# A two-layer trunk of four mixers: the scores of its linear attentions and of its RWKV chunks by halves of the array's rows

## The chip, the cores and the metric

The kernel runs on one core of one Trainium2 chip. The metric is the device time of one execution, in microseconds (us); the engines are TensorE (PE, with PEld for its weight loads), VectorE (DVE), ScalarE (ACT), GpSimd (POOL) and SyncE (SP), which issues most DMAs.

## What is computed

x has 512 tokens and 1024 channels. Each of two layers adds four mixers of 256 channels each, and then a gated feed-forward net:

```python
h = _rms_norm(x, norm_mix_pre[l])
p_a, p_b, p_c, p_d = _split(h @ w_in[l], (RWKV_COLS, GLA_COLS, LRU_COLS, HGRN_COLS))
y_a = _rwkv7_group(p_a, ...)    # delta-rule state, 4 heads of 64
y_b = _gla_group(p_b, ...)      # linear attention, 4 heads, keys of 32, values of 64
y_c = _rglru_group(p_c, ...)    # gated linear recurrence
y_d = _hgrn2_group(p_d, ...)    # linear attention, 4 heads, keys and values of 64
x = x + _rms_norm(jnp.concatenate([y_a, y_b, y_c, y_d], -1) @ w_out[l], norm_mix_post[l])
gate, up = jnp.split(_rms_norm(x, norm_ffn_pre[l]) @ ffn_w_gate_up[l], 2, axis=-1)
x = x + _rms_norm((jax.nn.silu(gate) * up) @ ffn_w_down[l], norm_ffn_post[l])
```

The two linear attentions share one recurrence; within a chunk their scores carry a decay per key channel:

```python
cum = jnp.cumsum(g_c, axis=-2)
diff = cum[:, :, :, None, :] - cum[:, :, None, :, :]
att = jnp.einsum('bhtk,bhsk,bhtsk->bhts', q_c, k_c, jnp.exp(jnp.where(causal, diff, -jnp.inf)))
o = jnp.einsum('bhts,bhsv->bhtv', att, v_c) + jnp.einsum('bhtk,bhkv->bhtv', q_c * jnp.exp(cum), S)
```

## The kernel before

Channels lie on the 128 partitions, tokens along the free dimension, so a tensor of 256 channels is two tiles of 128 x 512, called ct 0 and ct 1. The wide products (w_in, w_out, the feed-forward's two) are the matmuls g of line 398; each weight and each activation is split in a rounded part and a rest, and a product is three or so matmuls of 512 or 256 columns.

**The levels.** `linear()` serves GLA (nh = 4 heads of 32 keys, one tile of keys) and HGRN2 (nh = 2 heads of 64 per tile, two tiles). It builds the 128 x 128 scores of a group of tokens, held keys down and queries across in `att`, by doubling: at level B = 1, 2, 4, ... 64 the queries of every second block of B tokens meet the keys of the block before them. Level 1 is made of products that POOL forms and matmuls with two or four columns (`pp`, line 983; `dk`, line 955, is the diagonal). A level from 2 on goes per tile: ACT makes one copy `qr` of the level's 256 queries per head, scaled by a column `hsel` that is one on that head's key rows and zero on the others (line 994); PE multiplies the keys of all 128 rows with these masked queries (`lv`, line 999), for HGRN2 four matmuls of 128 columns into one PSUM bank, for GLA two banks of two matmuls of 256 columns; DVE copies the bank's valid places into `att` under a mask (line 1005; the last two levels ACT, by plain copies). Behind a level DVE multiplies the queries and the keys by the decay of their block (lines 1017 and 1018), in place. Since an f32 matmul is done in two passes, it shows as two records in the trace: HGRN2's 8 matmuls of a level are 16 records.

**The chunk products.** `rwkv()` has four heads of 64 channels, two to a tile, on rows 0 to 63 and 64 to 127. Line 656 multiplies a head's `bk` and `ar` for each of 8 chunks (64 rows x 128 columns, `A`), four of them into one PSUM bank, head after head, and DVE cuts four pieces out of each bank (lines 661 to 663). Later in `rwkv()`, blocks are transposed, applied and joined (`pq`, `px`, `py`, lines 829 to 843) into chunk outputs `Y` (lines 905 to 911), and Y's mean and variance per head are taken by two matmuls (`mean`, line 916, `var`, line 440) with an ACT step between them (line 918), before the `gate` of line 927.

**PSUM.** Eight banks: three for g (`pg`), three for `A` and most of RWKV (`pr`, taken by `psr`), two for the linear attentions (`pm`, by `psm`).

**The order.** The four mixers and the w_in products that fill PE are five generators, and `merge()` emits instructions by turns from one `yield` to the next. A string of digits per layer, ORDER, says whose turn it is (0 the w_in products, 1 RWKV, 2 HGRN2, 3 GLA, 4 the RG-LRU); what is left when a string ends goes by rates. A scheduler then places the emitted instructions on the engines' queues by its model of their times, so w_out's matmuls can come to stand between the last mixer steps. An engine runs its queue in order.

## Time and profile before

| what | value |
|---|---|
| median of 3 runs | 1410.99 us (1409.94 to 1411.83) |
| the profiled execution | 1410.65 us, of which the span is 1408.9 us |
| PE, PEld, DVE, ACT, POOL busy | 96%, 82%, 56%, 45%, 6% of the span |
| mixers of layer 0 and of layer 1 | about 85 to 290 us and 780 to 985 us of the span |
| line 994 (masked queries) | 96 instructions |

Times in the rows further below are in us from the start of the span. PE's two figures overlap, since a weight load runs beside the matmul before it. PE at 96% is a mean over stages: outside the mixers it is fed without a gap, inside them the stretches differ, and the change touches only the mixers.

### The profile page before, as it was taken

Reading aid. Unit: us, or ns where it says so; the run is one execution under the profiler, and the core shown is the slowest. Engines: PE = TensorE matmul, PEld = TensorE weight load, DVE = VectorE, ACT = ScalarE, POOL = GpSimd, SP = SyncE. Lnnn points to the kernel's source line nnn. Section 1 sums busy time; section 2 is a strip of 40 time slices with the busy share of each in tenths; the row PEclk is TensorE's granted clock in tenths of the full one; section 3 lists DMA queues with packets and bytes.
Section 4 is the critical chain, followed back from the end, with each engine's and each line's share of the span. In section 5 each row is a group of like instructions: output and inputs, shape, how many; then the busy total and the mean of one; then the engine's idle time right before and its main releaser. Section 6 shows DMA issues by size and latency. Waiting matters only on the chain.

```text
span 1408.9 us, 20225 instructions
## 1 busy us (share of the span) xinstructions
PE 1359.2 (96%) x8284; PEld 1150.8 (82%) x8284; DVE 792.9 (56%) x1241; ACT 633.5 (45%) x1035; POOL 81.0 (6%) x71
## 2 busy tenths in 40 slices
PE   7999998999999999999999999989999999999996
PEld 7877877779988888888897778776998888888886
DVE  7598848746834344412666996586286444433234
ACT  6546458555623232322556374676464232223232
POOL 0130102000000000000002300120000000000000
PEclk9989999999999999999999899999999999999999
DMA  7101202314422222433542111133053313233342
GB/s 269 59 30 30 75 16 90 92 46 135 165 90 90 75 90 75 145 91 94 173 149 60 45 45 61 40 96 107 24 171 116 124 45 114 70 101 121 106 130 85
DMA packets 51692, 131.75 MB, mean 94 GB/s; under 512 B 4752, under 2 KB 23776, under 8 KB 51600
## 3 DMA queue, kind: packets, MB, share of 16 engines
q1 hardware_dynamic: 50400, 128.47, 28.5%
q8 instruction: 65, 1.06, 0.3%
q10 hardware_dynamic: 960, 0.95, 0.2%
q0 software_dynamic: 240, 1.05, 0.2%
q14 instruction: 27, 0.22, 0.0%
HBM read 122.06 MB, written 8.39 MB: 93 GB/s over the span
## 4 chain that ended last, share of the span: by engine, by line
PE 79%; DVE 9%; ACT 8%; DMA 2%; issue 2%; POOL 0%; SPq 0%; DVEq 0%; ACTq 0%; POOLq 0%
PE g L398 69%; PE lv L999 2%; DMA block_ws<-in_w_in_dram 1%; DVE block_wl L389 1%; PE nrm L451 1%; ACT block_wh L388 1%; DVE block_att L1005 1%; DMA block_x<-in_xT_dram 1%; PE A L656 1%; PE px L836 1%; ACT block_ws L994 0%; PE ap L742 0%; DVE block_ws L1018 0%; PE pq L829 0%; ACT L1179 0%
## 5 line engine op out<-in xcount | busy, mean ns | idle before, releaser
L398 PE MATMUL g<-block_h,block_wh 128*128 128x512 f32 (+1 forms) x1738 | 496.7, 364 | 9.0 <-ACT block_h L479 7.6
L398 PEld LDWEIGHTS g<-block_h,block_wh 128*128 128x128 f32 x1738 | 317.1, 192 | 61.6 <-ACT block_h L479 8.1
L398 PE MATMUL g<-block_h,block_wl 128*128 128x512 f32 (+1 forms) x1126 | 340.8, 360 | 0.7 <-DVE block_wl L389 0.6
L398 PE MATMUL g<-block_wl,block_wh 128*128 128x512 f32 (+1 forms) x827 | 255.7, 353 | 0.2 <-ACT block_wh L388 0.2
L398 PEld LDWEIGHTS g<-block_h,block_wl 128*128 128x128 f32 x1126 | 210.3, 192 | 32.6 <-DVE block_wl L389 1.9
L388 ACT CAST block_wh<-block_ws 128x1024 fp32r<-128x1024 f32 (+1 forms) x124 | 128.4, 1038 | 226.2 <-DMA block_ws<-in_w_dn_dram 66.2
L398 PE MATMUL g<-block_wl,block_wl 128*128 128x512 f32 (+1 forms) x607 | 184.9, 351 | 0.0
L398 PEld LDWEIGHTS g<-block_wl,block_wh 128*128 128x128 f32 x827 | 151.4, 191 | 22.8 <-ACT block_wh L388 1.0
L389 DVE TENSOR_TENSOR block_wl<-block_ws,block_wh 128x1024 fp32r<-128x1024 f32 (+1 forms) x82 | 102.9, 1257 | 83.6 <-ACT block_wh L388 68.2
L398 PEld LDWEIGHTS g<-block_wl,block_wl 128*128 128x128 f32 x607 | 111.1, 190 | 15.4 <-issue 0.7
L388 ACT CAST block_wl<-block_ws 128x1024 fp32r<-128x1024 f32 (+1 forms) x46 | 47.4, 1031 | 93.6 <-PE g L398 35.4
L398 PE MATMUL g<-block_g,block_wl 128*128 128x512 f32 (+1 forms) x314 | 82.5, 344 | 0.0
L398 PE MATMUL g<-block_g,block_wh 128*128 128x512 f32 (+1 forms) x280 | 81.2, 347 | 0.0
L389 DVE TENSOR_TENSOR block_wl<-block_ws,block_wl 128x1024 fp32r<-128x1024 f32 (+1 forms) x32 | 38.1, 1191 | 50.1 <-ACT block_wl L388 45.8
L398 PEld LDWEIGHTS g<-block_g,block_wl 128*128 128x128 f32 x314 | 53.6, 189 | 7.2 <-issue 0.2
L398 PEld LDWEIGHTS g<-block_g,block_wh 128*128 128x128 f32 x280 | 48.6, 189 | 6.6 <-issue 0.2
L389 DVE TENSOR_TENSOR block_wh<-block_ws,block_wh 128x1024 fp32r<-128x1024 f32 (+1 forms) x29 | 34.6, 1192 | 32.8 <-ACT block_wh L388 27.2
L398 PE MATMUL g<-block_wh,block_wh 128*128 128x512 f32 (+1 forms) x145 | 46.6, 342 | 0.0
L398 PE MATMUL g<-block_wh,block_wl 128*128 128x256 f32 (+1 forms) x133 | 37.9, 337 | 0.4 <-DVE block_wl L389 0.4
L580 POOL TENSOR_SCALAR block_sq<-block_sq 64x512 f32<-64x512 f32 x2 | 1.2, 618 | 579.1 <-DVE block_cum L1250 521.2
L398 PE MATMUL g<-block_h,block_y 128*128 128x512 f32 x90 | 33.7, 389 | 0.0
L398 PE MATMUL g<-block_g,block_h 128*128 128x512 f32 (+1 forms) x100 | 33.0, 366 | 0.0
(1096 smaller groups left out, 2122.1 us busy)
## 6 DMA issues: line engine op xcount, KB each, us to landing
block_ws<-in_w_gu_dram SPq DMA_DIRECT2D x78, 512.0 KB, 3.6
block_ws<-in_w_in_dram SPq DMA_DIRECT2D x48, 512.0 KB, 3.7
block_ws<-in_w_dn_dram SPq DMA_DIRECT2D x39, 512.0 KB, 3.6
block_ws<-in_w_dn_dram SPq DMA_DIRECT2D x18, 384.0 KB, 3.1
xs<-block_x SPq DMA_DIRECT2D x18, 256.0 KB, 3.9
block_x<-xs SPq DMA_DIRECT2D x18, 256.0 KB, 4.0
block_x<-in_xT_dram SPq DMA_DIRECT2D x14, 256.0 KB, 5.3
block_ws<-in_w_out_dram SPq DMA_DIRECT2D x6, 512.0 KB, 3.7
```

What stands on the lines that cost most here:

```text
L388: nc.scalar.copy(out=wh, in_=ws)
L389: nc.vector.tensor_sub(out=wl, in0=ws, in1=wh.bitcast(F32))
L398: nc.tensor.matmul(ps, lhsT=w[:, i, :], rhs=h[i], start=(first and n == 0), stop=(last and n == len(steps) - 1))
L451: nc.tensor.matmul(ps, lhsT=self.ones, rhs=acc[:, s], start=(s == 0), stop=(s == 1))
L580: nc.gpsimd.tensor_scalar(out=low[64:128, :], in0=low[64:128, :], scalar1=0.5, scalar2=0.5, op0=ALU.mult, op1=ALU.add)
L656: nc.tensor.matmul(ps[:, j * P:(j + 1) * P], lhsT=bk[ct][p0:p0 + 64, c_ * P:(c_ + 1) * P], rhs=ar[ct][p0:p0 + 64, c_ * P:(c_ + 1) * P], st ...
L836: nc.tensor.matmul(ps[:, g * P:g * P + P], lhsT=n21[h][:, g * P:(g + 1) * P], rhs=pq[h][:, g * P:g * P + P], start=True, stop=True)
L999: nc.tensor.matmul(ps[:, j * nh * 64:(j + 1) * nh * 64], lhsT=Kt[ct][:, g * P:(g + 1) * P], rhs=qr[:, g].rearrange("p h c -> p (h c)"), st ...
L1005: nc.vector.copy_predicated(out=av[:, :, :, 1, :], mask=m, data=pv)
```

## The change

**Levels.** The 128 rows of keys are split in two halves of 64 rows. Two banks of `pm` are taken at once, one for each half, and the matmuls of a level go by turns: half 0 into the first bank, half 1 into the second (new line 1012). With HGRN2 a half is a head: 16 matmuls of 64 rows and 64 columns, both tiles of keys in one go, that read Q itself; no masked queries are made. With GLA a half holds two heads: 8 matmuls of 128 columns on two masked queries instead of four (new line 1002, by a new constant `hodd`). `att` is kept by halves instead of by tiles. Level 1 and the diagonal of both tiles share one PSUM tile. The branch for B = 2 with PPB, which was not taken, goes.

**Chunk products.** Per tile and per four chunks two `pr` banks are taken, and matmuls alternate between the two heads (new line 657).

**Order.** Both ORDER strings are new. Of line 994's 96 instructions 24 are left (line 1002); ACT loads a function table 41 times instead of 46 (four fewer in layer 0, one in layer 1), as RG-LRU steps that use one table come together. DVE's rows stay about the same (1193 instead of 1195). Matmuls of 64 rows come in 33 runs between others instead of 17. For the most part the halves do alternate; in layer 0 eight matmuls of `lv_5_16` and eight of `lv_5_17` stand one after the other with two `A` between, and GLA's second level of both layers is parted in the same way.

```diff
+    c["hodd"] = (p[:, None] // 32 % 2 == np.arange(2)[None, :])
...
-        for h in range(4):
-            ct, p0 = h // 2, 64 * (h % 2)
-            s_, k_, z_ = self.u("sr"), self.u("sak"), self.u("n21")
+        for ct in range(2):
+            new = [[self.u(n) for n in ("sr", "sak", "n21")] for _ in range(2)]
             for hf in range(2):
-                ps = self.psr("A")
+                pair = [self.psr("A") for _ in range(2)]
                 for j in range(4):
-                    c_ = hf * 4 + j
-                    nc.tensor.matmul(ps[:, j * P:(j + 1) * P], lhsT=bk[ct][p0:p0 + 64, c_ * P:(c_ + 1) * P],
-                                     rhs=ar[ct][p0:p0 + 64, c_ * P:(c_ + 1) * P], start=True, stop=True)
+                    cc = slice((hf * 4 + j) * P, (hf * 4 + j + 1) * P)
+                    for hh in range(2):
+                        rr = slice(64 * hh, 64 * hh + 64)
+                        nc.tensor.matmul(pair[hh][:, j * P:(j + 1) * P], lhsT=bk[ct][rr, cc], rhs=ar[ct][rr, cc], start=True, stop=True)
...
-            for ct in range(ncs if B > PPB else 0):
-                qr = (self.u if nh == 2 else self.u4)("qr").rearrange("p (g h c) -> p g h c", g=4, h=nh)
-                q4 = Q[ct].rearrange("p (g n s b) -> p g n s b", g=4, s=2, b=B)[:, :, :, 1, :]
-                for h in range(nh):
-                    nc.scalar.activation(out=qr[:, :, h, :].rearrange("p g (n b) -> p g n b", b=B), in_=q4, func=AF.Copy, scale=hsel[:, h:h + 1])
-                for bk in range(nbk):
-                    ps = self.psm("lv")
-                    for j in range(tpb):
-                        g = bk * tpb + j
-                        nc.tensor.matmul(ps[:, j * nh * 64:(j + 1) * nh * 64], lhsT=Kt[ct][:, g * P:(g + 1) * P],
-                                         rhs=qr[:, g].rearrange("p h c -> p (h c)"), start=True, stop=True)
...
+                q4 = [z.rearrange("p (g n s b) -> p g n s b", g=4, s=2, b=B)[:, :, :, 1, :] for z in Q]
+                if nh == 4:
+                    qr = self.u4("qr").rearrange("p (g h c) -> p g h c", g=4, h=4)[:, :, 0:2, :]
+                    for h in range(2):
+                        nc.scalar.activation(out=qr[:, :, h, :].rearrange("p g (n b) -> p g n b", b=B), in_=q4[0], func=AF.Copy, scale=self.c("hodd")[:, h:h + 1])
+                ps = [self.psm("lv") for _ in range(2)]
+                for i in range(8 if nh == 2 else 4):
+                    for half in range(2):
+                        rr = slice(64 * half, 64 * half + 64)
+                        ct, g = i // 4, i % 4
+                        if nh == 2:
+                            rhs, out = q4[ct][rr, g], ps[half][:, i * 64:i * 64 + 64].rearrange("p (n b) -> p n b", b=B)
+                        else:
+                            rhs, out = qr[rr, g], ps[half][:, i * P:i * P + P].rearrange("p (h c) -> p h c", h=2)
+                        nc.tensor.matmul(out, lhsT=Kt[ct][rr, g * P:(g + 1) * P], rhs=rhs, start=True, stop=True)
+                for half in range(2):
+                    av = halves[half]
...
                     if lv < 5:
-                        m = self.lmask[:, lv, :].rearrange("p (n b) -> p n b", b=B).unsqueeze(1).to_broadcast([P, 8, nb, B])
-                        nc.vector.copy_predicated(out=av[:, :, :, 1, :], mask=m, data=pv)
+                        nc.vector.copy_predicated(out=av[:, :, :, 1, :], mask=mask, data=pv)
```

The order of the work shows it at three places. The first is ACT in the tail of layer 0, where GLA's levels (the four-fold copies) meet RWKV's copies out of `pq`; L1179 is the RG-LRU's second gelu, with its table load. Before:

```order
L994 ACTIVATE block_ws_77_1593<-block_ws_10_288,cst 128x4x64 x4
L1179 ACT_TABLE_LOAD
L1179 ACTIVATE block_prw_2_4_218<-block_prw_2_4_218 128x512
L994 ACTIVATE block_qr_18_2082<-block_ws_10_288,cst 128x4x64
L831 COPY block_qr_23_1131<-pq_119_2019 128x512
L994 ACTIVATE block_qr_18_2082<-block_ws_10_288,cst 128x4x64 x3
L418 CAST block_y_21_2043<-block_ig_8_1009 128x512
L831 COPY block_qk_5_803<-pq_121_2025 128x512
L831 COPY block_sq_33_146<-pq_123_2069 128x512
L994 ACTIVATE block_qr_21_2122<-block_ws_10_288,cst 128x4x64 x4
L388 CAST block_wh_55_2550<-block_ws_54_2549 128x1024
L831 COPY block_prw_2_4_218<-pq_125_2091 128x512
```

After, at the same levels:

```order
L1002 ACTIVATE block_qr_15_2077<-block_sq_2_284,cst 128x4x64 x2
L418 CAST block_y_21_2057<-block_ig_8_1021 128x512
L834 COPY block_sak_50_1070<-pq_119_2033 128x512
L1002 ACTIVATE block_qr_18_2101<-block_sq_2_284,cst 128x4x64 x2
L834 COPY block_ws_10_288<-pq_121_2039 128x512
L388 CAST block_wh_55_2576<-block_bk_31_828 128x1024
L834 COPY block_prw_2_8_281<-pq_123_2091 128x512
L1002 ACTIVATE block_ws_42_940<-block_sq_2_284,cst 128x4x64 x2
L834 COPY block_prw_2_4_218<-pq_125_2115 128x512
L841 COPY block_sg_14_661<-px_127_2121 128x512
L1002 ACTIVATE block_qr_24_2190<-block_sq_2_284,cst 128x4x64 x2
```

A level has two masked queries instead of four, and the gelu with its load no longer stands among them.

The second place is PE at the end of layer 0, from RWKV's last chunk outputs `Y` on. Before:

```order
L911 MATMUL Y_4_162_2462<-block_n21_4_43_963,block_rs_4_20_676 64x64 x14
L916 MATMUL mean_4_164_2494<-block_ws_2_10_288,cst_75 128x512
L440 MATMUL var_4_166_2497<-block_plr1_3_40_927,cst_75 128x512
L927 MATMUL gate_4_168_2503<-block_sq_1_2_284,lowup_0_44_519 128x512
L398 MATMUL g_0_53_2548<-block_h_0_27_137,block_wh_0_55_2550 128x512
L398 MATMUL g_0_53_2548<-block_h_0_27_137,block_wl_0_56_2551 128x512
```

After, the end of the w_out matmuls that now stand between `Y` and the mean, the mean, and the first of those behind it:

```order
L398 MATMUL g_0_65_2643<-block_wh_3_73_1499,block_wh_0_67_2644 128x256
L398 MATMUL g_0_65_2643<-block_wh_3_73_1499,block_wl_0_68_2645 128x256
L919 MATMUL mean_4_164_2521<-block_pgl5_3_55_1114,cst_75 128x512
L398 MATMUL g_0_75_2708<-block_h_0_27_137,block_wh_0_77_2709 128x256
L398 MATMUL g_0_75_2708<-block_h_0_27_137,block_wl_0_78_2710 128x256
L398 MATMUL g_0_75_2708<-block_wh_3_91_1872,block_wh_0_77_2709 128x256
L398 MATMUL g_0_53_2575<-block_h_0_23_131,block_wh_0_55_2576 128x512
```

Before, mean, variance and gate follow each other; now 20 w_out matmuls stand between `Y` and the mean and 16 between the mean and the variance.

The third place is the same step at the end of layer 1. Before, from the last w_out matmuls ahead of the mean:

```order
L398 MATMUL g_0_464_8050<-block_wl_16_79_6973,block_wh_0_466_8051 128x256
L398 MATMUL g_0_464_8050<-block_wl_16_79_6973,block_wl_0_467_8052 128x256
L916 MATMUL mean_17_164_7922<-block_sq_14_2_5600,cst_75 128x512
L398 MATMUL g_0_474_8115<-block_h_12_2_5384,block_wh_0_476_8116 128x256
L398 MATMUL g_0_474_8115<-block_h_12_2_5384,block_wl_0_477_8117 128x256
L398 MATMUL g_0_474_8115<-block_y_20_19_7408,block_wh_0_476_8116 128x256
L398 MATMUL g_0_474_8115<-block_y_20_19_7408,block_wl_0_477_8117 128x256
```

After:

```order
L398 MATMUL g_0_464_8098<-block_wh_16_83_7060,block_wl_0_467_8100 128x256
L398 MATMUL g_0_474_8163<-block_wh_16_83_7060,block_wh_0_476_8164 128x256
L398 MATMUL g_0_474_8163<-block_wh_16_83_7060,block_wl_0_477_8165 128x256
L919 MATMUL mean_17_164_7971<-block_prw2_15_15_5744,cst_75 128x512
L440 MATMUL var_17_166_7974<-block_ws_0_354_4817,cst_75 128x512
L930 MATMUL gate_17_168_7980<-block_prw2_15_15_5744,lowup_0_437_5956 128x512
L398 MATMUL g_0_446_7998<-block_h_12_12_5518,block_wl_0_428_5356 128x512
```

Here it is the other way round: 16 w_out matmuls stood between mean and variance before, and none does now.

## Rows read from the trace of the kernel before

**Rows 1.** Busy time by stretch, layer 0: start:end, length, engines, PEclk, DMA share, GB/s.
```profile
85.00:112.00 27.00, 24.23 (x110) 19.98 (x109) 27.00 (x41) 9.43 (x17) 11.59 (x7) 0.81 0.09 36
112.00:123.00 11.00, 10.62 (x35) 8.39 (x36) 10.76 (x26) 4.35 (x11) 0.00 (x0) 0.70 0.00 0
...
159.00:200.00 41.00, 40.81 (x334) 32.68 (x336) 25.60 (x46) 18.92 (x35) 0.00 (x0) 1.00 0.17 53
...
226.00:246.00 20.00, 14.83 (x90) 13.21 (x89) 18.36 (x27) 18.36 (x38) 5.51 (x6) 0.91 0.40 132
246.00:265.00 19.00, 18.32 (x257) 16.15 (x256) 16.96 (x38) 7.82 (x14) 0.00 (x0) 1.00 0.31 87
```

**Rows 2.** The same view, layer 1, the two stretches of its tail.
```profile
911.00:929.00 18.00, 12.38 (x75) 9.08 (x74) 14.45 (x21) 13.79 (x25) 11.45 (x11) 0.96 0.45 147
929.00:953.00 24.00, 23.25 (x170) 21.24 (x171) 20.50 (x36) 15.60 (x31) 0.00 (x0) 0.89 0.22 66
```

**Rows 3.** PE timeline, 88 to 130: start, us, engine, line, operation, tiles, shape, count.
```profile
101.46 0.95 PE L955 MATMUL dk<-cst,block_qk 128*128 128x2 f32 x8
102.27 1.03 PE L983 MATMUL pp<-cst,block_qk 128*128 128x2 f32 x8
...
108.75 0.39 PE L398 MATMUL g<-block_h,block_wh 128*128 128x512 f32 x1
109.07 1.16 PE L656 MATMUL A<-block_x,block_x 64*128 64x128 f32 x8
110.15 1.05 PE L983 MATMUL pp<-cst,block_qk 128*128 128x2 f32 x8
...
126.61 0.39 PE L398 MATMUL g<-block_h,block_wl 128*128 128x512 f32 x1
126.84 1.05 PE L999 MATMUL lv<-block_ws 128*128 128x128 f32 x8
127.64 0.71 PE L398 MATMUL g<-block_h,block_wh 128*128 128x512 f32 x2
```

**Rows 4.** PE timeline, 62.4 to 64.6: two 32-row matmuls, each in two passes.
```profile
62.53 0.69 PE L589 MATMUL zw<-block_sq,lowup 32*128 32x512 f32 x1
62.53 0.69 PE L594 MATMUL za<-block_sq,lowup 32*128 32x512 f32 x1
```

**Rows 5.** PE timeline, 827.3 to 828.3: products of heads in different row halves.
```profile
827.40 0.71 PE L656 MATMUL A<-block_ar,block_bk 64*128 64x128 f32 x6
828.04 0.49 PE L999 MATMUL lv<-block_qr,block_ws 128*128 128x128 f32 x2
```

**Rows 6.** PE timeline, 218 to 264: the tail of layer 0, waits in brackets.
```profile
235.50 1.16 PE L829 MATMUL pq<-block_bmat,block_cum 128*128 128x128 f32 x8 [2.09 <-ACT block_qr L831]
...
248.19 1.89 PE L999 MATMUL lv<-block_qr,block_ws 128*128 128x256 f32 x8
249.92 1.05 PE L843 MATMUL py<-block_sq,block_cum 128*128 128x128 f32 x8
```

**Rows 7.** Stretches of both mixers, instructions of L994 alone: busy ACT (count).
```profile
85.00:290.00 205.00, 21.30 (x48) 0.95 0.19 59
780.00:985.00 205.00, 20.97 (x48) 0.96 0.21 68
```

**Rows 8.** ACT timeline, 222 to 262: the tail of layer 0.
```profile
226.74 1.78 ACT L994 ACTIVATE block_ws<-block_ws,cst 128x256 f32<-128x256 f32 x4 [2.56 <-DVE block_ws L1017]
...
232.52 1.28 ACT L1179 ACT_TABLE_LOAD   x1
```

**Rows 9.** DVE timeline, 222 to 262: masked copies and decays of one level.
```profile
251.19 1.30 DVE L1005 COPY_PREDICATED block_att<-lmask,lv 128x512 f32<-128x512 int32 x2
252.41 0.41 DVE L1018 TENSOR_TENSOR block_ws<-block_ws,block_sq 128x256 f32<-128x256 f32 x1
```

**Rows 10.** PE timeline, 279 to 291.5: the end of layer 0, waits in brackets.
```profile
285.44 1.12 PE L916 MATMUL mean<-block_ws,cst 128*128 128x512 f32 x2 [0.69 <-ACT block_ws L913]
288.38 1.12 PE L440 MATMUL var<-block_plr,cst 128*128 128x512 f32 x2 [1.82 <-ACT block_plr L918]
```

More of the change, by code (lines that the diff above doesn't have):

```diff
@@ L43 @@
 CONSTS = [("ident", 128), ("bones", 128), ("cent", 128), ("eye32", 32), ("eye64", 64), ("mnt", 128), ("mn21", 128), ("mak", 128),
[L44 removed]
+          ("mr", 64), ("m4", 32), ("m8", 32), ("m16", 32), ("m32", 32), ("scan", 512), ("hsel", 8), ("hodd", 2)]
 COFF = {}
@@ L97 @@
 KEEP = 0
-PPB = 1
 WIDE = True
@@ L664, in rwkv @@
-                yield
-            sr.append(s_)
-            sak.append(k_)
-            n21.append(z_)
+                for hh in range(2):
+                    s_, k_, z_ = new[hh]
+                    pv = pair[hh].rearrange("p (g s c) -> p g s c", g=2, s=4)
+                    for dst, m in ((nt[ct][:, hh, gg, :], "mnt"), (g4(k_)[:, gg, :], "mak"), (g4(z_)[:, gg, :], "mn21")):
+                        nc.vector.tensor_tensor(out=dst, in0=pv[:, :, 1:3, :].rearrange("p g s c -> p g (s c)"), in1=bc(self.c(m), 2), op=ALU.mult)
+                    nc.vector.tensor_tensor(out=s_.rearrange("p (g s c) -> p g s c", g=NPAIR, s=2)[:, gg], in0=pv[:, :, 0:4:3, :],
+                                            in1=self.c("mr").unsqueeze(1).unsqueeze(1).to_broadcast([P, 2, 2, 64]), op=ALU.mult)
+                    yield
@@ L669, in layouts @@
+            for s_, k_, z_ in new:
+                sr.append(s_)
+                sak.append(k_)
+                n21.append(z_)
         def layouts(ct):
@@ L946, in linear @@
         ncs = len(Q)
-        nbk = 1 if nh == 2 else 2
-        tpb = 4 // nbk
-        att, tots, tst, prod = {}, [], [], []
+        att, tots, tst, prod = [], [], [], []
+        by_half = lambda z: z.rearrange("p (h j) -> p h j", h=2)
+        if nh == 2:
+            place = lambda z, ct, g: by_half(z)[:, :, ct * 4 + g]
+        else:
+            place = lambda z, ct, g: by_half(z)[:, :, g * 2:g * 2 + 2]
+        pd = self.pm.tile([P, 16], F32, tag="pm", name=self.nm("dk"))
         for ct in range(ncs):
@@ L952, in linear @@
             nc.gpsimd.tensor_mul(out=qk[:, 0], in0=Q[ct], in1=Kt[ct])
-            pd = self.pm.tile([P, 4, nh], F32, tag="pm", name=self.nm("dk"))
             for g in range(4):
-                nc.tensor.matmul(pd[:, g, :], lhsT=qk[:, 0, g * P:(g + 1) * P], rhs=hsel, start=True, stop=True)
+                nc.tensor.matmul(place(pd, ct, g), lhsT=qk[:, 0, g * P:(g + 1) * P], rhs=hsel, start=True, stop=True)
             prod.append(qk)
-            dk = self.sp.tile([P, 4 * nh], F32, tag=f"dk{nh}{ct}", name=self.nm("dk"))
-            nc.scalar.copy(out=dk, in_=pd.rearrange("p g h -> p (g h)"))
-            for bk in range(nbk):
-                t = self.u4("att").rearrange("p (j c) -> p j c", c=P)
-                nc.gpsimd.tensor_tensor(out=t, in0=self.c("ident").unsqueeze(1).to_broadcast([P, 8, P]),
-                                        in1=dk[:, bk * 8:bk * 8 + 8].unsqueeze(2).to_broadcast([P, 8, P]), op=ALU.mult)
-                att[ct, bk] = t
             nc.vector.tensor_mul(out=Q[ct], in0=Q[ct], in1=F[ct])
@@ L966, in linear @@
             tst.append(self.u("tots"))
+        dk = self.sp.tile([P, 16], F32, tag=f"dk{nh}", name=self.nm("dk"))
+        nc.scalar.copy(out=dk, in_=pd)
+        for half in range(2):
+            t = self.u4("att").rearrange("p (j c) -> p j c", c=P)
+            nc.gpsimd.tensor_tensor(out=t, in0=self.c("ident").unsqueeze(1).to_broadcast([P, 8, P]),
+                                    in1=dk[:, half * 8:half * 8 + 8].unsqueeze(2).to_broadcast([P, 8, P]), op=ALU.mult)
+            att.append(t)
+        yield
+        if nh == 2:
             yield
@@ L990, in linear @@
[L990 to L1002 removed]
+            halves = [att[half].rearrange("p j (n s b) -> p j n s b", s=2, b=B) for half in range(2)]
```

49 lines of the change are left out of this document (21 added, 28 removed).

## The prediction

> **What bounds the kernel now.** I read the busy times by stretch first, since PE's mean of 96% hides the mixers. In layer 0 the limit changes [rows 1]: from 85 to 112 us DVE is busy 27.00 of 27 us, from 112 to 123 again 10.76 of 11; from 159 to 200 PE is busy 40.81 of 41; from 226 to 246 DVE and ACT are busy 18.36 each of 20 and PE only 14.83; from 246 to 265 PE has 18.32 of 19 and DVE 16.96. In layer 1 [rows 2], from 911 to 929 nothing is full (PE 12.38, DVE 14.45, ACT 13.79 of 18), which means that single waits in a chain set the time; from 929 to 953 PE is busy 23.25 of 24. So PE time is worth something where PE is full, ACT time where ACT is in the chain, and DVE, whose work the change leaves as it is, caps both: a stretch can't get shorter than its DVE time. Then I read PE's rows for the price of a pass, and ACT's, DVE's and PE's waits in the tails.
>
> **What a matmul costs.** In an f32 matmul of 128 columns a pass takes 0.11 us: eight of `dk` start at 101.46 and what follows at 102.27, so 0.81 for 8, and eight of `lv` stand from 126.84 to 127.64, 0.80 [rows 3]. `dk` moves two columns, `lv` 128, and the price is the same; what a pass of this kind pays is thus the load of 128 weight columns, not the columns that it moves. With 256 moving columns eight passes take 249.92 - 248.19 = 1.73, 0.216 each [rows 6]. Whether two row halves overlap is the question of the change. The two 32-row matmuls `zw` and `za`, on different rows and banks, both start at 62.53 and both last 0.69 [rows 4]; and six records of `A` that join two heads take 828.04 - 827.40 = 0.64 us [rows 5], no more than six full passes (0.66) though they are 64-row work, which alone takes 110.15 - 109.07 = 1.08 for 8, or 0.135 [rows 3]. I take a pair of halves to cost one pass, 0.11.
>
> A visit to the 64-row form has a price: 8 `A` take 1.08 where 8 `lv` take 0.80, so 0.28, and the `g` ahead of them is left after 0.32 (108.75 to 109.07) where it is left after 0.23 (126.61 to 126.84), so 0.09 [rows 3]; 0.37 together, for 16 more visits 5.9 us. The Trainium skill has a rule that speaks against the change here: "TensorEngine Tiling (Array Packing)", section Key Properties, says that changing the tiling mode drains the TensorE. The trace agrees with a price for it, 0.37 us by the rows, and I charge it by the rows.
>
> **PE's account.** HGRN2: 16 records of 0.11 = 1.76 us a level become 16 pairs of 0.11 = 1.76: nothing gained; where halves don't alternate it loses, some 2.5 us for the runs that I count in the new order. GLA: 8 records of 0.216 = 1.73 become 8 pairs of 0.11 = 0.88, so -0.85 for each of 12 levels of both layers, less for the three that are parted: 9 x 0.85 = -7.7. `A`: the 64 matmuls of both layers are 128 records, which become 64 pairs; 64 passes fewer at 0.80 / 8 = 0.10: -6.4. Visits +5.9. The sum is -5.7 us of PE. What counts is where.
>
> **ACT's account.** Line 994 is busy 21.30 us for 48 copies and 20.97 for 48 [rows 7], 0.44 each; 72 fewer are -31.6 us. Five table loads fewer at 1.28 [rows 8] are -6.4. Most of the 38 us lie in stretches where ACT isn't the limit.
>
> **Where it lands, layer 0.** 85 to 123: DVE is full, so `A` and HGRN2's copies are worth nothing; 0. 123 to 226: PE is full and gets nothing back from HGRN2; `A`'s half of 6.4 stands against eight visits (+3.0) and parted halves; 0. One table load lies on the chain of waits late in this part (ACT carries it from 200 to 226): -1.3. 226 to 246: ACT makes 20 copies here, half of which go, 10 x 0.44 = 4.4, with the gelu's load 5.7; PE waits 2.09 for ACT in it [rows 6], and a level's four copies take 1.78 [rows 8]. DVE's 18.36 of 20 caps it at -1.6. 246 to 265: three GLA levels, 3 x 0.85 less 3 x 0.37 = -1.4 (DVE's cap would be -2.0). After that, PE waits 0.69 for the mean's input and 1.82 for the variance's [rows 10]; the new order puts 20 and 16 w_out matmuls there, so -2.5. Layer 0: -1.3 - 1.6 - 1.4 - 2.5 = -6.8.
>
> **Layer 1.** The front as in layer 0: 0. 911 to 929: two of four copies (-0.9) and one table load (-1.3) of the chain: -2.2, within DVE's slack of 3.55. 929 to 953: PE full, four GLA levels, -3.4, four visits, +1.5: -1.9. At the end the same 16 matmuls have left the place between mean and variance, so the wait of 1.82 that layer 0 loses arises here: +1.8. Layer 1: -2.3.
>
> The sum is -9.1, from the profiled execution's 1410.65: 1401.5 us. The median of the runs, 1410.99, is 0.3 above that execution, so the forecast for the median is the same within its own error.
>
> **What can't be read.** Halves with 64 moving columns, alternating for 16 matmuls, no row shows. From below: a pair could cost as little as half a pass (0.055), from above two passes (0.22); the nearest row is `A` joining two heads [rows 5], which is one pass, and this I take. Reading Q with a stride instead of a packed copy I put at nothing, since passes are bound by the load; if it isn't, it costs at most the price of 0.216 of a pass with twice the columns. DVE's copies keep their shapes, 0.65 us each [rows 9].
>
> **Rivals.** *More of ACT counts.* If the chains through ACT are shortened by their full savings and DVE's stretches shrink as well since its inputs come earlier: three more table loads of layer 0 (-3.9), four copies more per tail, -5 each: 1401.5 - 14 = about 1387.5. For it speaks the wait of 2.56 us ahead of the copies at 226.74 [rows 8], against it DVE's full stretches [rows 1]. Chance 0.13.
>
> *HGRN2's levels halve, too.* If two halves of 64 rows load and move at once and 64 columns are cheaper than 128, a pair costs 0.055, and 12 levels gain 12 x 0.88 = -10.6, of which I let all count: about 1391. `dk` with two columns at the full 0.11 [rows 3] speaks against it. The Trainium skill, "TensorEngine Tiling (Array Packing)", section Theoretical Speedup, gives up to 2x where the contraction is 64 or less; by that rule, if it came on top of the columns, it would be this case. Chance 0.04.
>
> *Absorbed.* The tails are bound by DVE and by RWKV's own chain, and each saved wait is taken up by the next: only the waits at the end of layer 0 and a table load are won, less the one at the end of layer 1: -2, 1408.5. For it speaks DVE at 18.36 of 20 and 16.96 of 19 [rows 1]. Chance 0.19, of which 0.08 within 0.2%.
>
> *Slower: the HGRN2 level as one piece.* Before, the first bank of a level is done after half its matmuls (0.88 us), its mask copy runs beside the second half, and Q's decay waits only for the ACT copy, since PE reads `qr`. Now both banks end with the last pair (1.76), and the decays of Q (0.41 each [rows 9]) wait for the matmuls as well. The two copies and the decays are at the head of DVE's queue, where DVE is the full engine (85 to 123): RWKV's cuts of `A` and w_in's subtractions are queued behind. Price 0.88 + 2 x 0.41 = 1.7 us a level, 12 levels: +20, so 1421. It turns the result into a loss from 1.0 us a level on (12 x 1.0 = 9.1 + 2.8). Against it: the order has two streams more to put between, and the level's place was chosen anew. Chance 0.12.
>
> *Slower: halves don't overlap.* If the halves run one behind the other, an HGRN2 level costs 32 x 0.11 = 3.52, +21 us in all, GLA's -7.7 and `A`'s -6.4 are gone: some 1436. The rows of `zw`, `za` and of `A` across two heads speak against it [rows 4, 5]. Chance 0.03.
>
> **How the numbers follow.** A measurement of this kernel can tell about 0.2%, 2.8 us. The forecast, 1395 to 1407, has 0.49; more of ACT 0.13, HGRN2 halved 0.04, absorbed 0.19, the two slower ones 0.15. Faster by over 0.2% (below 1408.2): 0.49 + 0.13 + 0.04 + 0.11 = 0.77, less 0.02 for forecasts that end short of it: 0.75; within: 0.08 + 0.02 = 0.10; slower: 0.15. The range takes in the case of more ACT (1387.5) and the absorbed one (to 1412) and leaves the slower ones out.
>
> **What would show it.** In PE's timeline two `lv` of different halves start a few ns apart and an HGRN2 level lasts 1.76 us, a GLA level 0.88. ACT has 24 masked queries and 41 table loads. The tails shrink (226 to 265 by about 3 us, 911 to 953 by about 4), 159 to 200 stays; the wait ahead of `var` is gone in layer 0 and is 1.8 in layer 1. I would be wrong if pairs cost over 0.15, if DVE's waits for PE at the mask copies grow by over a us per level, or if the front of the mixers, where I expect nothing, moves by several us.

## The result: slower by half a per cent, where a gain was forecast

The changed kernel takes 1417.09 us (median of 15 runs, 1414.37 to 1425.83), the kernel before 1410.99 (15 runs beside them). The ratio is 1.0059 with an interval of 1.0046 to 1.0072: slower, about 8 us in the mean, where 9.1 us less were forecast. The changed kernel's runs lie at 1414 to 1419 us or at 1422 to 1426, the latter at a lower mean clock (0.970 to 0.971 instead of 0.974 to 0.980). The profiled execution took 1415.45 us, span 1413.6; the one of before 1410.65, span 1408.9.

The stretches of [rows 1, 2] in the changed kernel; the columns are start:end, length, busy time (and count) of PE, PEld, DVE, ACT and POOL, then PEclk, DMA share and GB/s:

```profile
85.00:112.00 27.00, 22.18 (x121) 18.19 (x120) 26.86 (x43) 6.07 (x9) 9.77 (x6) 0.87 0.21 75
112.00:123.00 11.00, 10.50 (x58) 8.19 (x58) 10.77 (x24) 1.45 (x2) 0.00 (x0) 0.84 0.01 1
159.00:200.00 41.00, 41.00 (x371) 33.49 (x370) 20.86 (x38) 16.83 (x30) 0.00 (x0) 1.00 0.13 40
226.00:246.00 20.00, 15.74 (x117) 14.17 (x116) 17.52 (x24) 11.66 (x25) 9.36 (x10) 0.91 0.32 105
...
929.00:953.00 24.00, 18.08 (x142) 16.89 (x141) 20.00 (x35) 11.88 (x24) 4.81 (x7) 0.75 0.14 42
```

ACT did fall where the copies were: 226 to 246 shows 11.66 us instead of 18.36. DVE is as full at the front as before. The last stretch now has PE at 18.08 of 24 and a clock of 0.75, where [rows 2] had 23.25 and 0.89. But equal times hold different work in the two kernels. For equal work I cut each layer in two: from the first w_in matmul of a layer's mixers to its last (the front), and from there to an equal place behind the mixers (the tail). PE's busy time of before in these four pieces, then of the changed kernel:

```profile
84.34:226.10 141.76, 137.01 (x889) 0.94 0.13 42
226.10:329.28 103.18, 94.00 (x900) 0.98 0.27 83
749.91:917.40 167.49, 163.39 (x984) 0.97 0.15 50
917.40:1009.13 91.73, 82.62 (x813) 0.96 0.23 72
```

```profile
84.47:228.90 144.43, 137.80 (x969) 0.92 0.14 44
228.90:329.64 100.74, 92.02 (x965) 0.98 0.26 78
751.11:921.20 170.09, 161.47 (x1081) 0.97 0.15 46
921.20:1013.83 92.63, 81.70 (x860) 0.93 0.21 66
```

In short windows PEclk reads either 1.00 or 0.50, the upper and the lower of its two levels (2.4 and 1.2 GHz). As an estimate, half of the busy time at the lower one is time that the clock took: six `g` of 512 columns from 139.40 to 141.96, at the lower level, take 0.43 us each, 24 from 163.54 on, at the upper, 0.24. I subtract it from the busy time and call the rest work:

| piece | elapsed | PE idle | taken by the clock | PE work |
|---|---|---|---|---|
| layer 0 front | 141.76 to 144.43 | 4.75 to 6.63 | 8.26 to 11.95 | 128.75 to 125.86 |
| layer 0 tail | 103.18 to 100.74 | 9.18 to 8.72 | 1.71 to 1.64 | 92.30 to 90.38 |
| layer 1 front | 167.49 to 170.09 | 4.10 to 8.62 | 5.12 to 4.18 | 158.27 to 157.29 |
| layer 1 tail | 91.73 to 92.63 | 9.11 to 10.93 | 2.91 to 3.87 | 79.71 to 77.84 |
| sum | 504.16 to 507.89 | 27.13 to 34.91 | 18.00 to 21.63 | 459.04 to 451.35 |

PE's work shrank by 7.7 us, more than the 5.7 forecast. It came back as 7.8 us more of waiting and 3.6 more at the lower clock: +3.7 us in the mixers, of the span's +4.7. A second profiled execution of the changed kernel (1418.97 us) has nearly the same work, 450.24, but 35.83 of waiting and 24.89 for the clock: 510.96 us in the mixers, +6.8.

**The prices are right.** PE of the changed kernel: start, duration, line, tiles, shape, count.

```profile
123.39 1.16 PE L657 MATMUL A<-block_ar,block_bk 64*128 64x128 f32 x16
124.48 0.73 PE L398 MATMUL g<-block_h,block_wh 128*128 128x512 f32 x2
...
161.61 1.11 PE L1012 MATMUL lv<-block_prw,block_ws 64*128 64x64 f32 x16
162.55 1.06 PE L1012 MATMUL lv<-block_pm 64*128 64x64 f32 x16
163.54 1.66 PE L398 MATMUL g<-block_h,block_wh 128*128 128x512 f32 x6
...
248.13 1.16 PE L1012 MATMUL lv<-block_qr,block_ig 64*128 64x128 f32 x16
249.22 1.16 PE L846 MATMUL py<-block_sg,block_cum 128*128 128x128 f32 x8
```

Sixteen records of `A` take 124.48 - 123.39 = 1.09, where eight took 1.08 [rows 3]. An HGRN2 level of 32 records takes 163.54 - 161.61 = 1.93 (1.76 forecast, without the way in), a GLA level 249.22 - 248.13 = 1.09 instead of 1.73 [rows 6], forecast 0.88 and 0.37 for the visit. ACT's masked copies (start:end, length, busy time of that line) fell from 21.30 and 20.97 us [rows 7] to

```profile
85.00:290.00 205.00, 5.49 (x12) 0.93 0.21 65
780.00:995.00 215.00, 5.47 (x12) 0.94 0.20 62
```

**The waits are new.** What PE waited for in the fronts of layer 0 and of layer 1 (engine, tile, line, releaser: us in all, times, longest):

```profile
PE lv L1012 <- DVE block_att L994: 2.4, 1, 2.4
PE dk L962 <- POOL block_qk L960: 1.9, 1, 1.9
PE lv L1012 <- DVE block_att L1017: 1.3, 2, 1.2
...
PE lg L1167 <- DVE block_att L994: 2.3, 1, 2.3
PE lv L1012 <- DVE block_att L1017: 1.5, 1, 1.5
PE lg L1167 <- DVE block_att L1017: 0.7, 1, 0.7
```

Lines 994 and 1017 are DVE's masked copies out of a `pm` bank. `lv` and `lg` don't read `att`; what they wait for is the bank. The five rows with `att` are 8.2 us (7.7 in the second execution); in the mixers of before no wait of PE that the view lists ended on a mask copy. They took the place of other waits (in layer 0's front before, 1.17 for a cut of `A` and 1.08 for a decay), so idle time rose by less.

Ahead of the first of them DVE, which is full here, stands still for two instructions beside HGRN2's diagonals of `att`, which POOL now forms one right behind the other (timelines of POOL and of DVE):

```profile
100.03 4.19 POOL L971 TENSOR_TENSOR block_att<-cst,dk 128x1024 f32<-128x1024 f32 x2
100.06 2.41 DVE L1161 SCALAR_TENSOR_TENSOR block_sq<-block_rs,vec,block_sq 128x511 f32<-128x511 f32 x1
102.39 2.91 DVE L389 TENSOR_TENSOR block_wh<-block_cum,block_wh 128x1024 fp32r<-128x1024 f32 x1
```

Instructions of these lines take 0.74 and 1.22 elsewhere in the front, so DVE lost 3.4 us. Before, it lost about as much beside the same two products, but 14 us apart.

In the tails the largest wait is now, in layer 0 and in layer 1,

```profile
PE pq L832 <- DVE block_cum L811: 4.3, 1, 4.3
...
PE pq L832 <- DVE block_phg L811: 5.9, 1, 5.9
```

The timeline of all engines of the changed kernel shows what made `pq` wait in layer 0 (waits in brackets):

```profile
232.19 0.56 POOL L826 COPY block_sq<-block_prw 64x256 f32<-64x256 f32 x1
...
232.41 4.34 DVE L1029 TENSOR_TENSOR block_sq<-block_sq,block_m 128x256 f32<-128x256 f32 x1
...
232.72 1.89 POOL L971 TENSOR_TENSOR block_att<-cst,dk 128x1024 f32<-128x1024 f32 x1
...
234.57 1.89 POOL L971 TENSOR_TENSOR block_pm<-cst,dk 128x1024 f32<-128x1024 f32 x1
236.67 1.17 DVE L811 COPY block_cum<-block_sak 32x256 f32<-32x256 f32 x4
...
237.99 0.77 PE L832 MATMUL pq<-block_qk,block_cum 128*128 128x128 f32 x2 [4.26 <-DVE block_cum L811]
```

The decay of 232.41 normally takes 0.41 us. It takes 4.34, and ends at 236.75, 0.3 us behind POOL's two broadcast products, GLA's diagonals of `att` (234.57 + 1.89 = 236.46). `pq`'s four copies stand behind it on DVE's queue. The Trainium skill, "SBUF — State Buffer", section Who interferes with whom, says that a DVE instruction with two inputs in SBUF contends with a GpSimd instruction that reads SBUF, and that the second to issue is blocked until the first is through. The trace agrees: POOL's copy of line 826 had been running for 0.22 us when the decay started, the two products followed it, DVE got no turn between them, and 0.41 us became 4.34.

In the kernel before layer 0's `pq` copies came ahead of the diagonals; in layer 1 the same stop was there already, and the forecast had not read it (timeline of before):

```profile
923.46 4.27 POOL L961 TENSOR_TENSOR block_att<-cst,dk 128x1024 f32<-128x1024 f32 x2 [3.31 <-issue]
923.99 4.49 DVE L808 COPY block_qr<-block_qr 32x256 f32<-32x256 f32 x4
...
928.62 0.77 PE L829 MATMUL pq<-block_bmat,block_qr 128*128 128x128 f32 x2 [4.12 <-DVE block_qr L808]
```

### The profile page after: what moved, and what is told of

Same layout as the page of the kernel before. It is cut to its first block, busy times and chain, and to the rows that moved or that the text cites. A ratio compares the mean times of both kernels' runs of the same rounds, so it can differ in the third digit from the quotient of the medians.

```text
span 1413.6 us, 20724 instructions
## 1 busy us (share of the span) xinstructions
PE 1355.2 (96%) x8572; PEld 1146.9 (81%) x8572; DVE 790.9 (56%) x1241; ACT 596.4 (42%) x956; POOL 78.8 (6%) x71
## 4 chain that ended last, share of the span: by engine, by line
PE 80%; DVE 11%; ACT 5%; DMA 2%; issue 1%; POOL 1%; SPq 0%; DVEq 0%; POOLq 0%; ACTq 0%
PE g L398 70%; PE lv L1012 2%; PE nrm L451 1%; PE pq L832 1%; DMA block_ws<-in_w_in_dram 1%; DVE block_wl L389 1%; DMA block_x<-in_xT_dram 1%; PE px L839 1%; DVE block_wh L389 1%; DVE block_att L1017 0%; DVE block_tots L1033 0%; PE ms L440 0%; PE o L1059 0%; ACT block_wh L388 0%; PE ap L745 0%
## 5 line engine op out<-in xcount | busy, mean ns | idle before, releaser
L398 PE MATMUL g<-block_h,block_wl 128*128 128x512 f32 (+1 forms) x960 | 290.9, 369 | 0.3 <-DVE block_wl L389 0.3
L398 PEld LDWEIGHTS g<-block_h,block_wl 128*128 128x128 f32 x960 | 184.1, 194 | 30.9 <-issue 1.4
L398 PE MATMUL g<-block_wl,block_wh 128*128 128x512 f32 (+1 forms) x710 | 204.3, 359 | 0.0
L398 PE MATMUL g<-block_g,block_wh 128*128 128x512 f32 (+1 forms) x415 | 120.8, 347 | 0.0
L398 PE MATMUL g<-block_wh,block_wh 128*128 128x256 f32 (+1 forms) x395 | 117.0, 332 | 0.4 <-DVE block_wh L389 0.4
L398 PE MATMUL g<-block_wl,block_wl 128*128 128x512 f32 (+1 forms) x358 | 108.1, 351 | 0.0
L398 PEld LDWEIGHTS g<-block_wh,block_wh 128*128 128x128 f32 x395 | 71.6, 191 | 7.8 <-DVE block_wh L389 0.6
L398 PEld LDWEIGHTS g<-block_wl,block_wl 128*128 128x128 f32 x358 | 65.8, 189 | 9.2 <-issue 0.2
L398 PE MATMUL g<-block_wh,block_wl 128*128 128x256 f32 (+1 forms) x240 | 72.5, 331 | 0.0
L398 PEld LDWEIGHTS g<-block_wh,block_wl 128*128 128x128 f32 x240 | 44.5, 190 | 4.9 <-issue 0.8
```

Source lines behind the costliest of these rows:

```text
L398: nc.tensor.matmul(ps, lhsT=w[:, i, :], rhs=h[i], start=(first and n == 0), stop=(last and n == len(steps) - 1))
```

## The experiments

**Parts of the change alone.** Four kernels take one part each, a fifth the new code with the old order.

```diff
 e1  before, with
+    pair = [self.psr("A") for _ in range(2)]     # and the loop over both heads of line 657
 e2  after, with linear() of before for HGRN2 (nh == 2)
 e3  after, with linear() of before for GLA (nh == 4)
 e4  before, with
-ORDER = ('0111101111011010210121241120...
+ORDER = ('0111101110111010210121241122...
 x   after, with the ORDER of before
```

The recorded expectations name theories. Theory 1, later B, is the HGRN2 level as one piece; theory 2, later A, is DVE standing still beside POOL's diagonals; theory 3 is the order strings. Theory C has the clock fall where the levels move few columns, theory D behind waits of PE.

> The kernel before with the chunk products of two heads alternating over two banks, and nothing else (old levels, old order string). Theory 1 (the HGRN2 level as one piece costs the time in the front of the mixers): the pairs are a pure gain of PE in stretches where DVE is the limit, so 0 to -4 us against before. Theory 2 (DVE is held up at the two diagonals formed by POOL, ahead of RWKV's blocks): the same, 0 to -4 us. Theory 3 (the new order string loses the time): 0 to -4 us. Above +2 us would say that the pairs themselves cost, for instance because two pr banks are held at once.

> The changed kernel with HGRN2's levels as before (masked queries, one tile at a time); pairs of chunk products, GLA by halves and the new order string stay. Theory 1 (HGRN2 as one piece): the loss in the front, 2.7 us in each layer, goes and the gain of GLA's levels stays: -5 to -9 us against before. Theory 2 (DVE held up at GLA's diagonals): the front comes back, the wait of pq (4.3 and 5.9 us in the changed kernel) stays: 0 to -4 us. Theory 3 (the order string): still +3 to +6 us.

> The changed kernel with GLA's levels as before (four masked queries, 256 columns); pairs of chunk products, HGRN2 by halves and the new order string stay. Theory 1 (HGRN2 as one piece): the loss in the front stays, the gain in GLA is gone: +6 to +12 us against before. Theory 2 (DVE held up at GLA's diagonals): those are formed in the same way, and GLA's old levels add 5 to 10 us in the tails: +5 to +12 us; if the wait of pq shrinks below 2 us here, theory 2 falls. Theory 3: +3 to +8 us.

> The kernel before, whole, with the new order strings alone. Theory 1 (HGRN2 as one piece) and theory 2 (DVE held up): within 3 us of before, since neither cause is in it. Theory 3 (the order string): +4 us or more.

> The new code with the old order strings. If each string fits only the code it was made for, as the old code with the new strings (+2.4%) suggests: +10 to +35 us against before. If the new code is better by itself and its new strings cost time: below the changed kernel, 1400 to 1412.

| kernel | median us | ratio to before |
|---|---|---|
| e1, chunk products alone | 1431.18 | 1.0161 (1.014 to 1.0183) |
| e2, GLA's levels and the chunk products | 1448.22 | 1.0275 (1.026 to 1.0291) |
| e3, HGRN2's levels and the chunk products | 1441.93 | 1.0218 (1.0185 to 1.0251) |
| e4, new order alone | 1443.10 | 1.0236 (1.0214 to 1.0258) |
| x, all but the new order | 1448.23 | 1.028 (1.0261 to 1.0299) |

Each is at least 14 us worse than either whole kernel, so none prices a part. The expectations for e1 to e3, between -9 and +12 us of before, were missed by far (22, 39 and 33); e4 came out as theory 3 has it (34), and x above its range (39). By e4 and x an order string fits only the code that it was made for. In e1 one and the same edit did nearly all of its harm in layer 1: ACT's table load of line 436 that comes some 290 us behind a layer's mixers is 1.0 us later than before in layer 0 (583.21 for 582.22) and 20.8 in layer 1 (1299.37 for 1278.59). Likewise x: its PE work in the mixers is 451.36, like the changed kernel's 451.35, but its idle time is 47.52 instead of 34.91 and the clock takes 43.60 instead of 21.63. All other experiments therefore freeze the order: the rows of each queue are recorded from the unedited kernel and imposed on the edited one, so that an edit changes durations and waits alone (where it takes an instruction to another engine or behind others, the text says so). Each result below is the median in us and the ratio to the kernel before, run beside it, with the 95% interval. The changed kernel itself, run again beside them, gives 1418.90, ratio 1.0062 (1.0045 to 1.0078):

> The changed kernel as it is, on the chip of this call, as the measure for the runs with its order kept: 1.004 to 1.008 of before, mean granted clock 0.975. A ratio below 1.003 would take the ground from the gain put down to the late diagonals and the doubled columns.

**Is the slower rival right, the HGRN2 level as one piece?** If the decays and mask copies behind a level's matmuls are what costs, it must help to let the matmuls read a constant instead of Q and K.

```diff
-rhs = q4[ct][rr, g];  lhsT = Kt[ct][rr, g * P:(g + 1) * P]
+rhs = f4[ct][rr, g];  lhsT = self.c("scan")[rr, g * P:(g + 1) * P]     # f4: the same view of scan; HGRN2 only
```

> The changed kernel, order kept, in which HGRN2's level matmuls read a constant instead of the decayed queries and keys (so no matmul waits for a decay and no decay for a matmul; the banks and the mask copies stay). Theory B (HGRN2's levels as one piece): the waits in the front go, -5 to -9 us against the changed kernel, to about 1408 to 1412. Theory A: within 2 us of the changed kernel. Theory C: within 2 us.

> The same edit in the kernel before, order kept: HGRN2's masked copies and level matmuls read a constant. Theory B: the levels were loose already, 0 to -2 us against before. Theory A and C: within 2 us of before. If it falls by as much as the same edit gives in the changed kernel, theory B falls.

After: 1417.97, 1.0058 (1.0043 to 1.0073), as without the edit, where theory B expected -5 to -9 us; before: 1409.21, 0.9989 (0.9975 to 1.0003). One half of this rival, which ended on the right side, is refuted: that decays and matmuls wait for each other costs nothing that can be measured in the changed kernel. The other half, mask copies that come only when both banks are done, the edit leaves as it is: PE's waits that end on a mask copy are still 7.8 us in the mixers.

**Do halves overlap?** Here both halves, of the levels and of `A`, go through rows 0 to 63.

```diff
-rr = slice(64 * half, 64 * half + 64)
+rr = slice(0, 64)
```

> The changed kernel, order kept, with all level matmuls and chunk products on rows 0 to 63 (the second half of keys is left out and the first taken twice), so that no two halves can run together. If pairs cost one pass by overlapping, PE's work rises by 12 x 1.76 for HGRN2, 12 x 0.88 for GLA and 64 x 0.11 for the chunk products, 39 us together, and the time by 25 to 40 us against the changed kernel. If the halves don't overlap, nothing changes. By theory D the time at the lower clock changes little.

1451.98, 1.03 (1.0276 to 1.0325). A level (PE timeline of this run):

```profile
174.64 2.00 PE L1012 MATMUL lv<-block_prw,block_ws 64*128 64x64 f32 x16
176.48 1.95 PE L1012 MATMUL lv<-block_pm 64*128 64x64 f32 x16
178.36 0.36 PE L745 MATMUL ap<-block_nst,block_m 128*128 128x32 f16 x8
```

178.36 - 174.64 = 3.72 instead of 1.93. So the overlap is real; that part of the forecast holds. PE's work in the mixers rises by 28 us to 479.41, less than the 39 expected; the clock takes 44.50 instead of 21.63 and PE waits 22.07 instead of 34.91. So not all of the 35 us is the price of a pass, and theory D, by which the clock would have changed little, is not borne out here.

**What is ACT's saving worth?** In the kernel before, the copies are made for one group of four only:

```diff
-out=qr[:, :, h, :], in_=q4          rhs=qr[:, g]
+out=qr[:, 0:1, h, :], in_=q4[:, 0:1]    rhs=qr[:, 0]
```

> The kernel before, order kept, with ACT's masked copies cut to one group of four (64 columns instead of 256; the level matmuls read that group for all four). It asks what ACT's saving alone is worth, with nothing else changed: 96 copies get shorter by 0.15 to 0.3 us, 15 to 29 us of ACT. By the prediction's account 2 to 5 us of that reach the end; by the rival in which all of ACT's saving in the tails counts, 6 to 12 us; if DVE and RWKV's chain absorb it, 0 to 1 us.

1404.31, 0.9965 (0.9949 to 0.9981): 5 us less, in the order of before and with nothing else changed. The copies got only 0.10 us shorter each (0.44 to 0.34), 10 us of ACT in all, so about half of what ACT saved reached the end.

**POOL's diagonals.** In both kernels (f3 after, f4 before) ACT writes the diagonal's place by a plain copy, and POOL's product goes.

```diff
-nc.gpsimd.tensor_tensor(out=t, in0=ident, in1=dk, op=ALU.mult)
+nc.scalar.copy(out=t, in_=ident)
```

> The changed kernel with every instruction in its old place on every queue, except that the eight diagonals of the scores are formed by ACT as plain copies of the unit matrix (the factor dk is left out) instead of by POOL. Theory A (DVE stands still while POOL forms the diagonals; in the trace one decay of 0.4 us takes 4.34 us beside them, ahead of RWKV's blocks): the wait of pq shrinks from 4.3 and 5.9 us to about 1 and 2, and the time falls by 5 to 8 us against the changed kernel, to about 1408 to 1412. Theory B (HGRN2's levels now run as one piece, copies and decays waiting for both banks): within 2 us of the changed kernel. Theory C (the slower clock in the front and the tail): within 2 us.

> The same edit in the kernel before, order kept: diagonals by ACT as copies of the unit matrix. Theory A: DVE is held up less there, since a layer's two HGRN2 diagonals were formed 14 us apart and pq's inputs came ahead of GLA's: 0 to -4 us against before, clearly less than the same edit gives in the changed kernel. Theories B and C: within 2 us of before.

After: 1407.11, 0.9994 (0.9974 to 1.0015), about 9 us better than the changed kernel (5 to 8 expected); before: 1405.93, 0.997 (0.9957 to 0.9982), 4 us better than its own. The place of layer 0 in f3's timeline:

```profile
228.29 0.62 DVE L1032 TENSOR_TENSOR block_sq<-block_sq,block_m 128x256 f32<-128x256 f32 x1
...
228.84 1.18 DVE L811 COPY block_cum<-block_sak 32x256 f32<-32x256 f32 x4
...
231.30 3.33 PE L832 MATMUL pq<-block_qk,block_cum 128*128 128x128 f32 x16
```

The decay takes 0.62 instead of 4.34 and `pq` doesn't wait. PE's idle time in the mixers falls from 34.91 to 23.43 us. The waits that end on a mask copy fall with it, from 8.2 to 4.3 us; the two for level 1's copies, 2.4 and 2.3, become 0 and 0.4. So a good part of them goes with the diagonals, and is not the price of the banks alone. Yet the front of layer 1 keeps 8.33 us of idle time, of 8.62. The profiled execution of f3, 7 us above its median, shows part of that given back to the clock (34.29 us). Between f3 and f4, both without the diagonals, the change still costs 0.9994 - 0.997 = 0.24%, 3.4 us, no more than the two intervals leave open.

If DVE makes the diagonals itself, nothing is won:

```diff
-nc.gpsimd.tensor_tensor(out=t, ...)
+nc.vector.tensor_tensor(out=t, ...)
```

> The changed kernel, whole, order kept, with the diagonals formed by DVE instead of POOL (nothing left out). Theory A (DVE is held for the whole of POOL's 4 us): DVE pays 2 x 1.2 us at each of the four places instead of standing still for 3 to 4 us, so -1 to -5 us against the changed kernel. If POOL's work was free beside DVE's: +2 to +8 us.

1417.92, 1.0061 (1.0046 to 1.0076), where -1 to -5 us were expected. Idle time is 30.71 us instead of 34.91 and 35.83 in the changed kernel's two profiled executions, but the clock takes 30.22 instead of 21.63 and 24.89.

Next only the time of GLA's diagonals moves: they wait for `pq`'s copies, and in layer 1 stand behind the POOL copies of lines 825 and 826. The same in the kernel before (h1).

```diff
+for i in gla_diagonals:
+    for e in pq_copies:      # line 811, in h1 808
+        tc.add_manual_dep(i, e.name, ...)
```

> The changed kernel, whole, order kept but for GLA's two diagonals of each layer: POOL forms them only after DVE has made the copies that pq needs (in layer 1 also after POOL's own copies for RWKV). Theory A (DVE held beside the diagonals): pq starts 3 to 4 us earlier in each layer; in layer 1 GLA's first mask copies now wait for the late diagonals, so 1 to 2 us come back: -3 to -7 us against the changed kernel, to about 1410 to 1414. If the place of the hold doesn't matter (it only meets DVE's work elsewhere): within 2 us of the changed kernel.

> The kernel before, whole, order kept, with GLA's diagonals waiting for the copies that pq needs. In layer 0 those copies come first anyway; in layer 1 they lie beside the diagonals and take 4.49 us instead of 1.2, so theory A expects -2 to -3.5 us against before (1406 to 1407.5). If the hold only meets other work of DVE: within 1 us of before.

After: 1414.59, 1.0036 (1.0019 to 1.0053), some 3.5 us better, an effect hardly larger than the intervals; `pq`'s wait falls from 4.26 to 0.54 us in layer 0 and from 5.9 to 1.6 in layer 1. Before: 1408.48, 0.9995 (0.9984 to 1.0006), no difference that can be told, where theory A expected -2 to -3.5 us, although the copies now take 1.17 instead of 4.49 us. The wait only moves on: PE waits 0.80 instead of 4.12 us for `pq`, but then 2.06 at the next half of a GLA level, for a mask copy that itself waits for the late diagonal (DVE in h1's timeline).

```profile
921.87 1.17 DVE L808 COPY block_qr<-block_qr 32x256 f32<-32x256 f32 x4
...
925.21 1.33 DVE L990 COPY_PREDICATED block_att<-lmask,pp 128x512 f32<-128x512 int32 x1 [1.44 <-POOL block_att L961]
```

**The clock.** In the changed kernel the clock falls twice among HGRN2's levels in layer 0. Four stretches of PE (length, busy, PEclk, DMA share, GB/s):

```profile
128.80:135.50 6.70, 6.70 (x43) 0.99 0.00 0
135.50:142.30 6.80, 6.80 (x28) 0.50 0.00 0
142.30:152.50 10.20, 8.88 (x90) 1.00 0.33 104
152.50:159.30 6.80, 6.80 (x32) 0.50 0.24 77
```

A run of levels and `A` begins in the first at 131.91, the levels end at 136.86; in the third a level follows on a wait of 1.15 us. PE is never idle in the second or the fourth. Two kernels let an HGRN2 matmul move 128 columns instead of 64: f7 all tokens of a group, f7b each column twice.

```diff
 f7
-rhs, out = q4[ct][rr, g], ps[half][:, i * 64:i * 64 + 64]
+rhs, out = Q[ct][rr, g * P:(g + 1) * P], ps[half][:, o:o + P]     # o = min(i * 64, 384)
 f7b, for i < 7
+rhs, out = q4[ct][rr, g].unsqueeze(1).to_broadcast([64, 2, nb, B]), ps[half][:, i * 64:i * 64 + P]
```

> The changed kernel, order kept, in which HGRN2's level matmuls move 128 columns instead of 64 (all queries of the group; what they write beyond their 64 columns is written over or left wrong). By the rows a pass is bound by its 128 weight columns, so the passes should keep 0.11 us a pair. Theory C (the granted clock falls because the new levels feed the array half as many columns in the same time): the time at the lower clock falls from 51 us in the mixers towards 38 us, the mean clock rises from 0.975 to 0.98 or more, and the time falls by 3 to 8 us against the changed kernel. Theory D (the clock falls behind waits of PE, not for what the matmuls carry): clock and time as in the changed kernel, within 2 us. If the passes get longer, by 12 levels of 16 pairs, the time rises by up to 20 us.

> The changed kernel, whole, order kept; HGRN2's level matmuls move their 64 columns twice (the second 64 are written over by the next matmul of the same half, the last one moves 64). It repeats the run with 128 columns without leaving anything wrong. Theory C (the clock falls where the levels feed few columns): mean clock 0.977 to 0.98 and -2 to -5 us against the changed kernel. Theory D (the clock falls behind waits alone): within 2 us, clock 0.975.

f7: 1414.72, 1.0039 (1.0027 to 1.0052). f7b: 1414.50, 1.0043 (1.0029 to 1.0058). Mean clock of the runs 0.9787 and 0.9792, against 0.9748 and 0.9758 for the changed kernel (15 and 4 runs) and 0.983 for the one before. A level costs nearly the same (f7: from 160.25 to 162.24, 1.99 us, against 1.93), and the first of the two falls is gone, while the second stays (f7b, PE):

```profile
128.40:135.10 6.70, 6.70 (x51) 1.00 0.00 0
135.10:141.90 6.80, 6.80 (x57) 1.00 0.01 2
...
147.25:154.08 6.83, 5.09 (x46) 0.50 0.38 146
```

Around the second, f7b's PE waits 2.42 us for DVE (line 735) and 1.74 for a mask copy. The edit brings 2.5 us, an effect about as large as the intervals: layer 0's front has 13.65 us at the lower level instead of 23.89, but 10.24 us of idle time instead of 6.63 in f7.

Late diagonals and doubled columns together:

> The changed kernel, whole, with both edits: late GLA diagonals and HGRN2's columns moved twice. If theories A and C hold and their gains add: -6 to -11 us against the changed kernel, 1406 to 1411, which is at or below the kernel before. If the clock gives back what the waits save, as when DVE formed the diagonals: -2 to -5 us.

1412.63, 1.0023 (1.0014 to 1.0032), clock 0.9813: 5 us better than the changed kernel and still slower than the one before. Only kernels that leave work out (f1, f4) were measurably faster than the kernel before.

## Why the prediction was wrong, point by point

- **Price of a pass and of a pair: right.** A pair of halves costs one pass (1.93 / 16 = 0.12 with the way in; 3.72 without the overlap). PE's work fell by 7.7 us, forecast 5.7; a GLA level at 1.09 instead of 0.88 + 0.37 puts a visit at 0.21, and 16 visits at 0.16 less are 2.6 us, about the difference.
- **ACT's account: right.** 24 copies of 0.46 us are left, ACT loads 41 tables, and f1 shows 5 us for shorter copies alone in the order of before.
- **"85 to 123: 0" and "123 to 226: 0, less a table load": wrong.** The front of layer 0 lost 2.67 us (forecast -1.3): work -2.9, idle +1.9, clock +3.7. "The front as in layer 0: 0" of layer 1 lost 2.6: work -1.0, idle +4.5, clock -0.9. The step that failed is the front put at nothing because DVE, then PE, is full there. In the sum, the two banks of `pm` that a level now takes at once got no term; the slower rival priced them with a chance of 0.12, and the prediction named growing waits at the mask copies as a sign of error. What the runs showed in place of the 0: PE waits for DVE's mask copies, 2.4 + 1.3 us in layer 0 and 2.3 + 1.5 + 0.7 in layer 1, and in layer 0 the clock takes 3.7 more. That a bank is what is waited for is read from the rows; no run with a third bank was tried, and in f3, without POOL's diagonals, 4.3 of these 8.2 us are left.
- **"226 to 265: -3.0", "the end: -2.5": half right.** The waits for `px`, mean and variance [rows 10] are gone, also the 2.09 for ACT [rows 6]; the tail of layer 0 shrank by 2.44 instead of 5.5. What took the rest is the 4.26 us that `pq` waits for DVE. This is the other step that failed, "DVE's 18.36 of 20 caps it at -1.6": it counts busy time as work, and the rows behind it include DVE standing still beside POOL, which the new order turned onto `pq`'s inputs. f3 shows it with -9 us (all diagonals gone from POOL); f8, which only makes GLA's diagonals late, with -3.5.
- **Layer 1, "-2.2 and -1.9, end +1.8": wrong.** The tail is 0.9 us longer with 1.9 us less work: `pq` waits 5.9 instead of 4.1, `dot` 1.8 instead of 0.5, and the clock takes 1.0 more. At the end the variance waits 0.69 where 1.8 was forecast, and 0.57 for the other tile.
- **The clock got no term.** The mean clock fell from 0.983 to 0.975; f7 and f7b give back 2.5 us of it, hardly clear of the intervals. Half-row matmuls with 64 columns were costed as time on PE alone.
- **The slower rival** gave the sign, but of its price of 1.7 us a level the decays' part (0.82) is at zero by f5_after. Its other part, mask copies behind both banks, is what the waits above look like, at 8.2 us in all instead of 12 x 0.88 = 10.6; it stays untested.

Of the 17 us between forecast and result, f3 against f4 puts about 5 on the diagonals (9 against 4; the intervals leave some 4 either way), f7 2.5 on the clock behind HGRN2's levels; f8 and f7b, 3.5 and 2.3 alone, are 5 together (f9), which is clear of the intervals. The larger part has no run that prices it. Open remains how much the bank waits cost by themselves, and how much is the order's: the strings alone move the time by some 30 us (e4, x), more than every part.

## What to carry to other kernels

Before counting an engine's busy time as work, look for instructions that last ten times their usual time, and name what runs beside them: a change that merely shifts order can put the same stop in front of the critical product. Work taken off PE can be lost again if the buffers it fills come free later than before, so count the banks that a step holds at once. And an order tuned for one code is no control for another: freeze the order before pricing a part.
